# Attention bias and mask: from matmuls into the score PSUM to factors applied after the exponential

## The chip, the cores and the metric

The kernel runs on all 8 cores of one Trainium2 chip. The metric is the device time of the slowest core, in microseconds. Before the change it is 1325.45 us (median of the 3 runs made first, 1325.04 to 1452.33; with a fourth run of 1325.14 us the median is 1325.3). A program on all 8 cores has a second, slower state: one die runs at a lower granted TensorE clock and the time is some per cent longer. The 1452.33 us run was in it. (Medians are quoted over all runs of a kernel: in runs 1, 3, 5, 7, 13 and 14 below one slow run is among them. Ratios leave the slow runs out.)

## The reference, cut to what matters

One layer of a streaming encoder: a half-step feed-forward network (FFN1), a mixing stage (attention beside a convolution, joined by an output projection), a second half-step feed-forward network (FFN2), a norm. The change touches only the scores of the attention.

```python
BATCH, SEQ, D_MODEL, CHUNK, LEFT_CHUNKS = 4, 4096, 1024, 64, 8
BAND = (LEFT_CHUNKS + 1) * CHUNK   # 576 keys per chunk of 64 queries
N_HEADS, HEAD_DIM, MAX_REL = 8, 64, 128
# inside chunk_band_attention(q, k, v, rel_bias); rel_bias: (2*MAX_REL+1, N_HEADS)
idx = jnp.clip(qi + LEFT_CHUNKS * CHUNK - kj, -MAX_REL, MAX_REL) + MAX_REL
bias = jnp.transpose(rel_bias[idx], (2, 0, 1))          # (H, CHUNK, BAND)
s = jnp.einsum('bcqhd,bckhd->bchqk', qc, kb) * scale
s = s + bias[None, None]
s = jnp.where(valid, s, NEG_INF)
p = jax.nn.softmax(s, axis=-1)
o = jnp.einsum('bchqk,bckhd->bcqhd', p, vb)
```

Because exp(s + b) = exp(s) exp(b), the bias can be added before the exponential or multiplied in after it. Distances of 128 or more share one bias value. Both kernels subtract that value from the whole table, which softmax doesn't notice, so only the 256 nearest columns of the band need any work.

## The kernel before

Each core takes half of one sequence, in two groups of blocks of 512, 384 or 256 frames (even cores: 512/384/256, then 512/256/256). Per group it runs FFN1, the mixing stage, FFN2. The order of all instructions is fixed when the program is built. An emitter keeps an estimated clock for each engine and each buffer, and always emits the piece of work that it expects to be ready first.

An attention *unit* is two heads (`e` = 0, 1) times up to 4 x 128 score columns (a "bin" of key tiles, each with the queries that see it). TensorE computes the unit's scores into one of two PSUM slots. ScalarE takes their exponential into one of four bf16 buffers, `Pb`. TensorE multiplies these by the values (PV; the 65th column gives the row sum). VectorE divides by the sum into `On`, TensorE transposes `On`, and the output projection follows. The head dimension is 64, so score matmuls use half of TensorE's rows, the two heads in the two halves ("64*128" in the profile, against "128*128"). Bias and mask are matmuls of half an identity with a table, into the same PSUM slot:

```python
def qk(u):                                   # scores of one unit
    sp_ = nxt("gub", 2)                      # PSUM slot
    for (r, a, w, o_) in u["lst"]:           # key tile r, w columns
        for e in range(2):
            lhsT, kk = kslice(kt0 + r, e, j)
            ops.append((e, lhsT, qT[e*64:e*64+64, j, m0+a:m0+a+w], o_, w, ...))
    for (r, a, w, o_) in u["lst"]:           # bias and mask, by matmul
        parts = []
        if r >= 3:                           # near the diagonal: bias
            q0 = (r - 4) * 128
            for half_, lim in ((0, 192), (1, 256)):
                lo, hi = max(a, q0), min(a + w, q0 + lim)
                parts.append((half_, B_BT + j*BW + 192*half_ + lo - q0, o_ + lo - a, hi - lo))
        if r < nt:                           # a key chunk too old: NEG
            parts.append((0, B_M0, o_ + r*128 - a + 64, 64))
        for half_, tb, c_, w_ in parts:
            for e in range(2):
                z = B_ID + 64 * (1 - half_ + e)
                ops.append((e, cb[64*e:64*e+64, z:z+128], cb[64*e:64*e+64, tb:tb+w_], c_, w_, ...))
    # ... emit all ops, accumulating in PSUM
    pi = nxt("Pb", 4)
    act(Pb[pi][:, :, 0:w], src, AF.Exp, 2 * w, ...)

def pv_at():                                 # when PV of the oldest unit may come
    if c == a: return INF
    return max(P.est("pe", (("P", u["pi"]),)), ob_free() if u["bi"] == 0 else 0.0)

def evac_engine(gi):                         # who empties the PSUM of projections
    if ("attn0", gi) in F and ("attn", gi) not in F:
        return "dve"                         # during attention: always VectorE
    return "act" if P.t["act"] < P.t["dve"] else "dve"

def rdy():                                   # gate/up of an FFN (fi == 1: FFN2)
    if fi == 1 and ("attn", gi) not in F: return INF
    # ...

def keep_warm(gap, skip):                    # dummy matmuls into an expected TensorE gap
    if gap < 0.8 or gap > 100: return
    # ...
```

Projections of later blocks are emitted between the units, as filler for TensorE. The sum of squares for the next norm is squared on ScalarE and added up on GpSimd (128x512 fp32 adds) during the attention. `On` lies in memory that FFN2's gate tile uses again.

The softmax here doesn't subtract the row's maximum and nothing guards it: scores larger than these inputs give would overflow.

Of the kernel before, what the change touches and what calls it, by code (L numbers as in the profile page):

```python
# [15 lines left out]
NEG = -30000.0  # L16
# [28 lines left out]
CS_RB = CS_LNB + NG  # L45
CS_N = CS_RB + 4
BW = 448
CB_BG = 0
CB_ID = 4 * BW
CB_IC = CB_ID + 256  # L50
CB_B5 = CB_IC + CH
CB_N = CB_B5 + 128
B_BT = 0
B_ID = 4 * BW
B_M0 = B_BT + 192
B_ONES = B_ID + 256
B_ONE5 = B_ONES + 128
B_N = B_ONE5 + 128

RING_COLS = 18736  # L60
D_BYTES = 49920
# [222 lines left out]
def build_nc(debug=None):  # L284
# [20 lines left out]
    with ExitStack() as es:  # L305
# [77 lines left out]
        onesS = cb[:, B_ONES:B_ONES + 128]  # L383
        id128 = cb[:, B_ID + 64:B_ID + 192]
        ones5 = cb[:, B_ONE5:B_ONE5 + 128]

        def make(half):
# [557 lines left out]
            def ffn(g, fi):  # L945
# [5 lines left out]
                for hf, npc in ((0, 6), (1, 5)):  # L951
# [22 lines left out]
                    def rdy():  # L974
                        if fi == 1 and ("attn", gi) not in F:
                            return INF
                        c = cand()
                        return min(x[0] for x in c) if c else INF
# [43 lines left out]
                    if hf == 1:  # L1022
                        for s in blocks:
                            F.add(("hfree", gi, idx + 1, s))
                    nf = 2 * npc
                    nm = "dA" if hf == 0 else "dB"
                    if hf == 0:
# [326 lines left out]
            def attention(g):  # L1354
# [5 lines left out]
                for s in g.fine:  # L1360
# [32 lines left out]
                    def qk(u):  # L1393
                        sp_ = nxt("gub", 2)
                        u["sp"] = sp_
                        j = u["j"]
                        ops = []
                        for (r, a, w, o_) in u["lst"]:
                            for e in range(2):
                                lhsT, kk = kslice(kt0 + r, e, j)  # L1400
                                ops.append((e, lhsT, qT[e * 64:e * 64 + 64, j, m0 + a:m0 + a + w], o_, w,
                                            (kk, ("q", gi, j, s)), w / 4800.0 + 0.0025))
                        for (r, a, w, o_) in u["lst"]:
                            parts = []
                            if r >= 3:
                                q0 = (r - 4) * 128
                                for half_, lim in ((0, 192), (1, 256)):
                                    lo, hi = max(a, q0), min(a + w, q0 + lim)
                                    parts.append((half_, B_BT + j * BW + 192 * half_ + lo - q0, o_ + lo - a, hi - lo))
                            if r < nt:  # L1410
                                parts.append((0, B_M0, o_ + r * 128 - a + 64, 64))
                            for half_, tb, c_, w_ in parts:
                                for e in range(2):
                                    z = B_ID + 64 * (1 - half_ + e)
                                    ops.append((e, cb[64 * e:64 * e + 64, z:z + 128], cb[64 * e:64 * e + 64, tb:tb + w_],
                                                c_, w_, ("cb",), w_ / 4800.0 + 0.0025))
                        left = [sum(1 for x in ops if x[0] == e) for e in range(2)]
                        seen = [0, 0]
                        for (e, lhsT, rhs, o_, w, rd, dur) in ops:
                            seen[e] += 1  # L1420
                            fin = seen[e] == left[e]
                            mm(2 * sp_ + e, o_, lhsT, rhs, w, seen[e] == 1, fin, rd, fin, dur=dur)
                        pi = nxt("Pb", 4)
                        u["pi"] = pi
                        w = u["n"]
                        src = ps4[:, sp_ * 1024:(sp_ + 1) * 1024].rearrange("p (e t) -> p e t", e=2)[:, :, 0:w]
                        act(Pb[pi][:, :, 0:w], src, AF.Exp, 2 * w, (("ps", 2 * sp_), ("ps", 2 * sp_ + 1)), (("P", pi),))

                    def pv(u):
# [40 lines left out]
                    def rdy0():  # L1470
                        if ("silu", gi) not in F or ("K", gi) not in F or ("Q", gi, s) not in F or ("v", gi, s) not in F or len(mode["lru"]) < 3 and len(ob) < nb:
                            return INF
                        b = 2 * nxt("gub", 2, False)
                        return P.est("pe", (("q", gi, 0, s), ("v", gi, kt0 + nt - 1)), (("ps", b), ("ps", b + 1)))
# [15 lines left out]
                    def pv_at():  # L1490
                        if c == a:
                            return INF
                        u = units[c]
                        return max(P.est("pe", (("P", u["pi"]),)), ob_free() if u["bi"] == 0 else 0.0)
# [86 lines left out]
            def setup_tables():  # L1581
                yield lambda: P.est("dve", ("stage",)) if all(("h", 0, 0, s) in F for s in G[0].ids) else INF
                dve(lambda h: h.tensor_copy(out=cb[:, B_ID:B_ID + 256], in_=stage[:, CB_ID:CB_ID + 256]), 256,
                    ("stage",), ("cb",))
                dve(lambda h: h.tensor_scalar(out=ic_t, in0=stage[:, CB_IC:CB_IC + CH], scalar1=0.5, scalar2=None,
                                              op0=ALU.mult), CH, ("stage",), ("ic",))
                dve(lambda h: h.tensor_scalar(out=ones5, in0=stage[:, CB_B5:CB_B5 + 128], scalar1=1.0 / 512, scalar2=None,
                                              op0=ALU.mult), 128, ("stage",), ("cb5",))
                for j in range(4):
                    rbc = cs[:, CS_RB + j:CS_RB + j + 1]  # L1590
                    for lo, hi in ((0, 192), (256, BW)):
                        src = stage[:, CB_BG + j * BW + lo:CB_BG + j * BW + hi]
                        dst = cb[:, B_BT + j * BW + lo:B_BT + j * BW + hi]
                        dve(lambda h, dst=dst, src=src, rbc=rbc: h.tensor_scalar(
                            out=dst, in0=src, scalar1=rbc, scalar2=None, op0=ALU.subtract), 192,
                            ("stage", "cs"), ("cb",))
                    m_ = cb[:, B_BT + j * BW + 192:B_BT + j * BW + 256]
                    dve(lambda h, m_=m_: h.memset(m_, NEG), 64, (), ("cb",))
                    yield lambda: P.t["dve"] - 1.0
                F.add(("tables",))  # L1600

            dve(lambda h: h.memset(onesS, 1.0 / 1024), 128, (), ("cb1",))
# [82 lines left out]
def _prep_shared(inp):  # L1685
# [44 lines left out]
    rb = np.asarray(inp["rel_bias"], f)[0]  # L1730
    cs[:, CS_RB:CS_RB + 4] = np.repeat(rb[256].reshape(4, 2).T, 64, axis=0)
    out["cs"] = cs
# [5 lines left out]
    for h in range(8):  # L1738
        c0, r0 = CB_BG + (h // 2) * BW, 64 * (h % 2)
        tab = rb[dist, h]  # L1740
        cbig[r0:r0 + 64, c0:c0 + 192] = tab[0:64, 0:192]
        cbig[r0:r0 + 64, c0 + 192:c0 + BW] = tab[64:128]
    cbig[:, CB_ID + 64:CB_ID + 192] = np.eye(128, dtype=f)
    cbig[:, CB_IC:CB_IC + CH] = np.tile(np.eye(CH, dtype=f), (PH, 1))
# [54 lines left out]
```

## Time and profile before

| what | before |
|---|---|
| time, median of all four runs (fast ones alone: 1325.14) | 1325.3 us |
| even cores, odd cores, span in the profile | 1321.5 to 1323.3, 1317.3 to 1318.3 us |
| granted TensorE clock by core | 0.994 to 0.997 |
| attention stage of group 0, of group 1 (core 6) | 70.1 and 73.6 us |
| bias and mask matmuls on core 6 | 456 |

All profile lines are of core 6. It is the slowest of the eight before, after and in run 1; in run 3 it is 0.4 us and in run 12 1.8 us below the slowest. From the page: busy time of each engine, and the chain that ended last.

```profile
PE 1292.1 (98%) x8666; PEld 740.4 (56%) x8666; DVE 487.1 (37%) x899; ACT 407.0 (31%) x727; POOL 229.0 (17%) x266
...
PE 92%; DVE 3%; DMA 2%; issue 1%; ACT 1%; SPq 0%; DVEq 0%; POOL 0%; ACTq 0%; POOLq 0%
```

TensorE (PE) sets the time: the chain runs 92% through it. Now the windows of the two attention stages, each from its first score matmul to its last transposes. The columns are start:end, length, then busy time and instructions of PE, weight load, VectorE, ScalarE and GpSimd, then granted clock, DMA share and GB/s.

```profile
357.80:428.00 70.20, 69.41 (x877) 43.57 (x877) 34.19 (x81) 48.06 (x68) 12.58 (x11) 1.00 0.20 48
999.50:1073.20 73.70, 72.01 (x985) 48.12 (x985) 34.57 (x80) 53.99 (x76) 13.04 (x13) 1.00 0.17 42
```

TensorE looks full here too: 2.5 us of 143.9 are not busy. VectorE is busy for less than half, ScalarE for about 70%. The groups that the change removes (count, then busy us and mean ns of one):

```profile
L561 PE MATMUL psA<-cb_sb 64*128 64x64 bf16 x144 | 12.1, 189 | 0.0
L561 PE MATMUL psA<-cb_sb 64*128 64x256 bf16 x88 | 12.0, 269 | 0.0
L561 PE MATMUL psA<-cb_sb 64*128 64x192 bf16 x88 | 10.8, 243 | 0.0
L561 PE MATMUL psA<-cb_sb 64*128 64x128 bf16 x136 | 10.4, 216 | 0.0
```

The means are of no use as costs. A 64-column matmul shows 189 ns and a 256-column one 269 ns, because each record spans the whole pipeline and overlaps its neighbours. What a matmul costs is read from start to start. Part of the TensorE timeline (start, length, group, count):

```profile
386.38 0.39 PE L561 MATMUL psA<-dreg,at 64*128 64x384 bf16 x4
386.61 0.36 PE L561 MATMUL psA<-cb_sb 64*128 64x64 bf16 x8
386.81 0.33 PE L561 MATMUL psA<-dreg,at 64*128 64x384 bf16 x2
386.97 0.35 PE L561 MATMUL psA<-cb_sb 64*128 64x192 bf16 x4
```

The matmuls come in pairs, one for each head; the second starts 3 ns after the first. A row of this view bears the form of its first matmul only: the eight of the second row are two of 64 and six of 128 columns. They take from 386.61 to 386.81 us. In the trace itself, the 64-column pair takes 28 ns and each 128-column pair 56. Last, what TensorE waits for over the whole span (total us, times, longest), and the end of the attention of group 1:

```profile
PEld ps L561 <- issue: 19.5, 46, 2.5
...
PE ps L561 <- DVE dreg L1456: 1.5, 2, 0.8
...
PE ps L561 <- ACT pb L574: 0.5, 1, 0.5
```

```profile
1067.63 1.91 PE L561 MATMUL ps<-dreg,ring 128*128 128x256 bf16 x16 [0.30 <-DVE xres L1556]
1069.37 3.98 PE L561 MATMUL psA<-hT,ring 128*128 128x512 bf16 x16
1073.18 0.27 PE L561 MATMUL ps<-cb_sb,dreg 128*128 128x128 bf16 x2
```

PV waits for an exponential (`ACT pb`) for 0.5 us in all, and transposes wait for `On` (`DVE dreg L1456`) for 1.5 us. In the second fence, FFN2's first tile (`psA<-hT,ring`, 16 matmuls) starts at 1069.37, ahead of the last transposes at 1073.18: it fills the time in which VectorE finishes the last block.

### The profile page before, as it was taken

What the parts mean: (1) busy time and instruction counts of PE and PEld (TensorE: products, weight loads), DVE (VectorE), ACT (ScalarE), POOL (GpSimd) and SP (SyncE); (2) the same over time, 40 slices, a digit from 0 to 9 for tenths busy, and PEclk for the clock granted to TensorE, in tenths of its full rate; (3) what the DMA queues carried; (4) which work ended last, traced back from release to release, by engine and by line L of the source; (5) the groups of instructions that cost most, each with busy time, mean ns of one, the idle gap of its engine ahead of it and who ended that gap; (6) DMA issues with size and microseconds to landing.
All of it is one profiled execution on the core that took longest, in us unless ns stands there. A gap on an engine that the chain in (4) does not pass through costs nothing.

```text
span 1323.3 us, 23324 instructions; the slowest of 8 cores (1317.3 to 1323.3 us)
## 1 busy us (share of the span) xinstructions
PE 1292.1 (98%) x8666; PEld 740.4 (56%) x8666; DVE 487.1 (37%) x899; ACT 407.0 (31%) x727; POOL 229.0 (17%) x266
## 2 busy tenths in 40 slices
PE   7999999999999999999999999999999999999995
PEld 3655655566665666665564444446566664444444
DVE  4522222263745522222266222125455362222125
ACT  3411011242666421001236110114338661101123
POOL 2263000341003320000161000014120220000022
PEclk9999999999999999999999999999999999999998
DMA  8795226244930753243445844342784125433503
GB/s 187 164 217 116 49 47 120 42 127 142 193 70 2 188 91 72 53 76 53 73 52 101 218 80 82 66 76 49 171 208 103 34 39 111 75 65 64 112 0 130
DMA packets 33923, 129.55 MB, mean 98 GB/s; under 512 B 2832, under 2 KB 13200, under 8 KB 26896
## 3 DMA queue, kind: packets, MB, share of 16 engines
q0 software_dynamic: 18752, 97.33, 38.9%
q1 hardware_dynamic: 15056, 30.68, 6.8%
q8 instruction: 73, 1.20, 0.4%
q14 instruction: 42, 0.34, 0.1%
HBM read 193.54 MB, written 18.68 MB: 160 GB/s over the span
## 4 chain that ended last, share of the span: by engine, by line
PE 92%; DVE 3%; DMA 2%; issue 1%; ACT 1%; SPq 0%; DVEq 0%; POOL 0%; ACTq 0%; POOLq 0%
PE psA L561 53%; PE ps L561 39%; DVE hT L823 1%; DMA gscr_1<-dreg 1%; DMA ring<-wgu 1%; DVE xres L1048 1%; DVE xres L823 0%; DMA dreg<-gscr_1 0%; ACT L569 0%; DMA xres<-xin 0%; ACT rstd L574 0%; SPq L1673 0%; DVE xres L1556 0%; ACT pb L574 0%; POOL ssb L771 0%
## 5 line engine op out<-in xcount | busy, mean ns | idle before, releaser
L561 PE MATMUL psA<-hT,ring 128*128 128x512 bf16 (+2 forms) x3792 | 691.4, 344 | 1.7 <-DVE dreg L1139 1.0
L561 PEld LDWEIGHTS psA<-hT,ring 128*128 128x128 bf16 x3792 | 370.6, 98 | 316.1 <-issue 3.6
L574 ACT ACTIVATE dreg<-psA 128x512 f32<-128x512 f32 (+3 forms) x279 | 162.3, 587 | 688.1 <-PE psA L561 678.6
L561 PE MATMUL ps<-at,ring 128*128 128x512 bf16 (+2 forms) x1920 | 326.6, 332 | 0.0
L1014 DVE TENSOR_TENSOR at<-psA,dreg 128x512 bf16<-128x512 f32 (+2 forms) x213 | 130.1, 612 | 450.7 <-PE psA L561 427.3
L561 PEld LDWEIGHTS ps<-at,ring 128*128 128x128 bf16 x1920 | 187.6, 98 | 137.2
L1048 DVE SCALAR_TENSOR_TENSOR xres<-ps,xres 128x512 f32<-128x512 f32 (+2 forms) x160 | 88.5, 556 | 168.0 <-PE ps L561 168.0
L766 POOL TENSOR_TENSOR ssum<-ssum,sq 128x512 f32<-128x512 f32 (+2 forms) x102 | 103.2, 1012 | 169.4 <-ACT sq L574 165.6
L668 POOL DMA_DIRECT2D ring<-wgu x47 | 25.6, 546 | 522.9 <-PE ps L561 261.0
L561 PE MATMUL ps<-dreg,ring 128*128 128x256 bf16 (+4 forms) x704 | 85.7, 274 | 2.1 <-DMA dreg<-gscr_1 1.5
L574 ACT ACTIVATE sq<-xres 128x256 bf16<-128x256 f32 (+2 forms) x108 | 55.3, 519 | 99.8 <-DVE xres L1048 66.7
L823 DVE SCALAR_TENSOR_TENSOR hT<-xres,cs_sb,rstd 128x256 bf16<-128x256 f32 (+2 forms) x120 | 70.4, 644 | 12.4 <-ACT rstd L574 12.4
L561 PEld LDWEIGHTS ps<-dreg,ring 128*128 128x128 bf16 x704 | 55.2, 98 | 23.1 <-issue 4.4
L561 PE MATMUL ps<-hT,ring 128*128 128x512 bf16 (+2 forms) x352 | 63.4, 336 | 0.0
L561 PEld LDWEIGHTS ps<-hT,ring 128*128 128x128 bf16 x352 | 33.6, 98 | 25.5 <-issue 0.4
L569 ACT ACT_TABLE_LOAD x36 | 46.2, 1283 | 0.6
L574 ACT ACTIVATE pb<-psA 128x1024 bf16<-128x1024 f32 (+2 forms) x42 | 37.7, 915 | 8.1 <-PE psA L561 7.9
L1556 DVE TENSOR_TENSOR xres<-ps,xres 128x256 f32<-128x256 f32 (+2 forms) x48 | 24.9, 531 | 37.2 <-PE ps L561 37.1
L1576 POOL TENSOR_TENSOR dreg<-pb 128x2560 bf16<-128x2560 bf16 x8 | 35.8, 4502 | 0.7 <-DMA cwscr<-dreg 0.7
L668 POOL DMA_DIRECT2D ring<-wdA x16 | 8.6, 537 | 135.7 <-PE psA L561 135.3
L561 PE MATMUL ps<-at,hT 128*128 128x512 bf16 x136 | 30.8, 379 | 0.0
L561 PE MATMUL psA<-cb_sb 64*128 64x64 bf16 (+3 forms) x456 | 27.8, 223 | 0.0
(93 smaller groups left out, 588.5 us busy)
## 6 DMA issues: line engine op xcount, KB each, us to landing
ring<-wgu POOLq DMA_DIRECT2D x41, 1024.0 KB, 8.4
ring<-wdA POOLq DMA_DIRECT2D x16, 768.0 KB, 8.6
ring<-wdB POOLq DMA_DIRECT2D x16, 640.0 KB, 7.9
ring<-cwscr POOLq DMA_DIRECT2D x16, 640.0 KB, 9.7
cwscr<-dreg SPq DMA_DIRECT2D x8, 640.0 KB, 6.1
ring<-wab POOLq DMA_DIRECT2D x8, 512.0 KB, 8.2
ring<-wout POOLq DMA_DIRECT2D x4, 1024.0 KB, 14.7
dreg<-xin SPq DMA_DIRECT2D x2, 2048.0 KB, 21.9
```

Source lines behind the costliest of these rows:

```text
L561: P.op("pe", lambda h: h.matmul(o, lhsT=lhsT, rhs=rhs, start=start, stop=stop, skip_group_check=True), (max(n / 2400.0 + 0.0025, 0.03) if ...
L569: P.op("act", lambda h: h.activation(out=cs[0:1, CS_N + i:CS_N + i + 1], in_=onesS[0:1, 0:1], func=func), 1.5, ("cb1",), ())
L574: P.op("act", lambda h: h.activation(out=out, in_=in_, func=func, **kw), 0.12 + n / 1200.0 + (0.09 * sum(isinstance(v, bass.AP) for v in k ...
L668: P.dma("pool", lambda h, dst=dst, src=src: h.dma_start(out=dst, in_=src), wtok(p, i), (256 if p.reads else 512) * w, reads=p.reads, after ...
L766: pool(lambda h: h.tensor_tensor(out=ss, in0=ss, in1=sqt, op=ALU.add), n, (sk, ("sq", i)), (sk,))
L823: dve(lambda h, dst=dst, xin=xin, gcol=gcol: h.scalar_tensor_tensor(out=dst, in0=xin, scalar=gcol, in1=rt, op0=ALU.mult, op1=ALU.mult), n, ...
L1014: dve(lambda h: h.tensor_tensor(out=at, in0=ub, in1=tt, op=ALU.mult), n, (("ps", bU), ("tmpF", ti)), (("AT", gi, fl, s),))
L1048: dve(lambda h, xo=xo, xi=xi, bk=bk: h.scalar_tensor_tensor(out=xo, in0=bk, scalar=0.5, in1=xi, op0=ALU.mult, op1=ALU.add), n, (("ps", b), ...
L1556: dve(lambda h, xo=xo, bk=bk: h.tensor_tensor(out=xo, in0=bk, in1=xo, op=ALU.add), n, (("ps", b),) + rk, (("x", gi, dm, s),))
L1576: P.op("pool", lambda h, o_=o_, i0=i0: h.tensor_tensor(out=o_, in0=i0, in1=i1, op=ALU.mult), 4.5, ("cmp", "ic", "cb"), (("cwb", i % 2),))
```

## The change

Intent: TensorE sets the time, so the 456 bias and mask matmuls go. Their work moves to VectorE, which is busy for 37%. The exponentials are multiplied in place by a bf16 table `eb` = exp(bias - far bias), and masked corners are set to zero. PV of a unit may be emitted only after its multiply. As one consequence FFN2 must wait until the last transposes of its group have been emitted, since its gate tile overwrites `On`. The diff, cut to its core (left out: the new layout of the constants, that the attention also waits for `eb`, and that `eb` is set to zero where a key lies in a later chunk than the query):

```diff
                     def rdy():
-                        if fi == 1 and ("attn", gi) not in F:
+                        if fi == 1 and (("attn", gi) not in F or any(("O", gi, 3, x) not in F for x in g.fine)):
                             return INF
@@ qk
-                        for (r, a, w, o_) in u["lst"]:
-                            parts = []
-                            ... (bias and mask matmuls, as printed above)
@@ after the exponential
+                        u["ok"] = False
+                        def weigh(u=u, pi=pi, j=j, nt=nt):
+                            for (r, a, w, o_) in u["lst"]:
+                                if r >= 3:
+                                    q0 = (r - 4) * 128
+                                    lo, hi = max(a, q0), min(a + w, q0 + 256)
+                                    x = Pb[pi][:, :, o_ + lo - a:o_ + hi - a]
+                                    y = eb[:, 2 * j:2 * j + 2, lo - q0:hi - q0]
+                                    dve(lambda h, x=x, y=y: h.tensor_tensor(out=x, in0=x, in1=y, op=ALU.mult),
+                                        2 * (hi - lo), (("P", pi), "eb"), (("P", pi),), rate=1900.0)
+                                if r < nt:
+                                    c_ = o_ + r * 128 - a + 64
+                                    z = Pb[pi][0:64, :, c_:c_ + 64]
+                                    dve(lambda h, z=z: h.memset(z, 0.0), 128, (), (("P", pi),))
+                            u["ok"] = True
+                        if any(r >= 3 or r < nt for r, a, w, o_ in u["lst"]):
+                            later(lambda pi=pi: P.est("dve", (("P", pi),)) - 0.3, (), weigh)
+                        else:
+                            u["ok"] = True
@@ pv_at
-                        if c == a:
+                        if c == a or not units[c]["ok"]:
@@ setup_tables
                 # ...
+                for h_ in range(8):
+                    # ...
+                    act(eb[:, h_, :], stage[:, CB_BG + 256 * h_:CB_BG + 256 * h_ + 256], AF.Exp, 256, ("stage",), ("eb",))
+                table(AF.Silu)
                 # ...
```

More of the change, by code (lines that the diff above doesn't have):

```diff
@@ L45 @@
 CS_RB = CS_LNB + NG
-CS_N = CS_RB + 4
-BW = 448
+CS_N = CS_RB + 8
 CB_BG = 0
-CB_ID = 4 * BW
-CB_IC = CB_ID + 256
+CB_ID = 8 * 256
+CB_IC = CB_ID + 128
 CB_B5 = CB_IC + CH
@@ L53 @@
 B_BT = 0
-B_ID = 4 * BW
-B_M0 = B_BT + 192
-B_ONES = B_ID + 256
+B_ID = 8 * 256
+B_ONES = B_ID + 128
 B_ONE5 = B_ONES + 128
 B_N = B_ONE5 + 128
-RING_COLS = 18736
+RING_COLS = 18592
 D_BYTES = 49920
@@ L383, in build_nc @@
         onesS = cb[:, B_ONES:B_ONES + 128]
-        id128 = cb[:, B_ID + 64:B_ID + 192]
+        id128 = cb[:, B_ID:B_ID + 128]
+        eb = cb[:, B_BT:B_BT + 2048].rearrange("p (h t) -> p h t", h=8)
         ones5 = cb[:, B_ONE5:B_ONE5 + 128]
@@ L1025, in ffn @@
                     nf = 2 * npc
+                    F.add(("down", gi, fi))
                     nm = "dA" if hf == 0 else "dB"
@@ L1402, in qk @@
                                             (kk, ("q", gi, j, s)), w / 4800.0 + 0.0025))
-                        for (r, a, w, o_) in u["lst"]:
-                            parts = []
-                            if r >= 3:
-                                q0 = (r - 4) * 128
-                                for half_, lim in ((0, 192), (1, 256)):
-                                    lo, hi = max(a, q0), min(a + w, q0 + lim)
-                                    parts.append((half_, B_BT + j * BW + 192 * half_ + lo - q0, o_ + lo - a, hi - lo))
-                            if r < nt:
-                                parts.append((0, B_M0, o_ + r * 128 - a + 64, 64))
-                            for half_, tb, c_, w_ in parts:
-                                for e in range(2):
-                                    z = B_ID + 64 * (1 - half_ + e)
-                                    ops.append((e, cb[64 * e:64 * e + 64, z:z + 128], cb[64 * e:64 * e + 64, tb:tb + w_],
-                                                c_, w_, ("cb",), w_ / 4800.0 + 0.0025))
                         left = [sum(1 for x in ops if x[0] == e) for e in range(2)]
@@ L1470, in rdy0 @@
                     def rdy0():
-                        if ("silu", gi) not in F or ("K", gi) not in F or ("Q", gi, s) not in F or ("v", gi, s) not in F or len(mode["lru"]) < 3 and len(ob) < nb:
+                        if ("eb",) not in F or ("silu", gi) not in F or ("K", gi) not in F or ("Q", gi, s) not in F or ("v", gi, s) not in F or len(mode["lru"]) < 3 and len(ob) < nb:
                             return INF
@@ L1582, in setup_tables @@
                 yield lambda: P.est("dve", ("stage",)) if all(("h", 0, 0, s) in F for s in G[0].ids) else INF
-                dve(lambda h: h.tensor_copy(out=cb[:, B_ID:B_ID + 256], in_=stage[:, CB_ID:CB_ID + 256]), 256,
-                    ("stage",), ("cb",))
+                dve(lambda h: h.tensor_copy(out=id128, in_=stage[:, CB_ID:CB_ID + 128]), 128, ("stage",), ("cb",))
                 dve(lambda h: h.tensor_scalar(out=ic_t, in0=stage[:, CB_IC:CB_IC + CH], scalar1=0.5, scalar2=None,
@@ L1588, in setup_tables @@
                                               op0=ALU.mult), 128, ("stage",), ("cb5",))
-                for j in range(4):
-                    rbc = cs[:, CS_RB + j:CS_RB + j + 1]
-                    for lo, hi in ((0, 192), (256, BW)):
-                        src = stage[:, CB_BG + j * BW + lo:CB_BG + j * BW + hi]
-                        dst = cb[:, B_BT + j * BW + lo:B_BT + j * BW + hi]
-                        dve(lambda h, dst=dst, src=src, rbc=rbc: h.tensor_scalar(
-                            out=dst, in0=src, scalar1=rbc, scalar2=None, op0=ALU.subtract), 192,
-                            ("stage", "cs"), ("cb",))
-                    m_ = cb[:, B_BT + j * BW + 192:B_BT + j * BW + 256]
-                    dve(lambda h, m_=m_: h.memset(m_, NEG), 64, (), ("cb",))
-                    yield lambda: P.t["dve"] - 1.0
-                F.add(("tables",))
+                for h_ in range(8):
+                    src, rbc = stage[:, CB_BG + 256 * h_:CB_BG + 256 * h_ + 256], cs[:, CS_RB + h_:CS_RB + h_ + 1]
+                    dve(lambda h, src=src, rbc=rbc: h.tensor_scalar(
+                        out=src, in0=src, scalar1=rbc, scalar2=None, op0=ALU.subtract), 256,
+                        ("stage", "cs"), ("stage",))
+                    if h_ % 2:
+                        yield lambda: P.t["dve"] - 1.0
+                F.add(("tables",))
+                for h_ in range(8):
+                    yield lambda: P.t["act"] - 0.5 if ("down", 0, 0) in F else INF
+                    act(eb[:, h_, :], stage[:, CB_BG + 256 * h_:CB_BG + 256 * h_ + 256], AF.Exp, 256, ("stage",), ("eb",))
+                table(AF.Silu)
+                dve(lambda h: h.memset(eb[64:128, :, 0:64], 0.0), 512, (), ("eb",))
+                F.add(("eb",))
             dve(lambda h: h.memset(onesS, 1.0 / 1024), 128, (), ("cb1",))
@@ L1730, in _prep_shared @@
     rb = np.asarray(inp["rel_bias"], f)[0]
-    cs[:, CS_RB:CS_RB + 4] = np.repeat(rb[256].reshape(4, 2).T, 64, axis=0)
+    cs[:, CS_RB:CS_RB + 8] = rb[256]
     out["cs"] = cs
@@ L1738, in _prep_shared @@
     for h in range(8):
-        c0, r0 = CB_BG + (h // 2) * BW, 64 * (h % 2)
-        tab = rb[dist, h]
-        cbig[r0:r0 + 64, c0:c0 + 192] = tab[0:64, 0:192]
-        cbig[r0:r0 + 64, c0 + 192:c0 + BW] = tab[64:128]
-    cbig[:, CB_ID + 64:CB_ID + 192] = np.eye(128, dtype=f)
+        cbig[:, CB_BG + 256 * h:CB_BG + 256 * h + 256] = rb[dist, h]
+    cbig[:, CB_ID:CB_ID + 128] = np.eye(128, dtype=f)
     cbig[:, CB_IC:CB_IC + CH] = np.tile(np.eye(CH, dtype=f), (PH, 1))
```

## The prediction

> **What bounds the kernel now.** TensorE. The page of the slowest core (6) has PE busy 1292.1 of 1323.3 us (98%), VectorE 37%, ScalarE 31%; the chain of waits is 92% PE. Clocks are granted at 0.994 or more; even cores (half 0) are about 4 us longer than odd ones. Time falls only where PE work falls and nothing else becomes the limit.
>
> **Removed.** The bias and mask matmuls (psA from cb_sb): 456 on core 6, 440 on core 7. Their 27.8 us in the groups view overlap neighbours. From start to start of consecutive matmuls in the trace they take 45 to 46 ns each, about 20.4 us of PE time, half in each attention stage (about 358 to 428 and 1000 to 1068 us). That is 1.5% of the span and a ceiling: over 2% (26.5 us) cannot come from it.
>
> **Added.** VectorE, between exponential and PV: I count 88 bf16 multiplies on core 6 (44 of 2x256, 44 of 2x128 elements) and 52 memsets of 2x64. The trace has no bf16 tensor_tensor on VectorE. The Trainium skill ("VectorE: DVE Perf Modes", The perf-mode tier table) gives it double rate from SBUF; no run here shows it yet. Estimate from this trace: fp32-to-bf16 casts within SBUF take 427 ns at 512 and 313 ns at 288 elements, so about 0.42 and 0.29 us; memset 165 ns for 128 elements. Sum: 18.5 + 12.8 + 8.6 = 40 us, 20 per stage. At single rate (0.69 and 0.42 us) it would be 57.
> Also 8 small exponentials and a table pair on ScalarE (about 6 us, in the first down projection, where ScalarE idles), and FFN2 waits for the last transposes. Ring offsets of the weights come out unchanged.
>
> **On the critical path.** The windows view of 1000 to 1074 has PE 72.3, ACT 54.3, DVE 34.6 us busy; 358 to 430 has PE 71.0, ACT 48.1, DVE 36.0. Without bias matmuls PE needs about 62 and 61; ACT stays, DVE rises to about 55. PE stays the largest, but the slack shrinks from 20 us to below 10 and each unit's chain gains a hop of 0.3 to 0.8 us. Four P buffers and projection matmuls as filler hide most of it. Weak places: the first 512-block of group 1 (1005 to 1028 us: 20 exponentials of 1.017 us in a stretch that would shrink to 22 us), and the tail of each group (exp, multiply, PV, reciprocal, transpose, output projection in series).
> I expect 65 to 75% of 20.4 us to survive, 14 us, less 2 us for the tails and the later FFN2 start: 12 to 13 us.
>
> **Prediction: 1313 us, 8 in 10 between 1306 and 1322.** Faster by over 2%: 0.02; within 2%: 0.94; slower by over 2%: 0.04.
>
> **What would show each step.** PE matmuls down by 456 on core 6; span down about 12 us, all in the two attention stages; FFN stages of unchanged length. New VectorE multiplies of 0.42 and 0.29 us; VectorE busy up about 40 us. PV matmuls waiting on VectorE for some us in total, PE idle in the attention stages up from about 3 us to 6 to 11. ACT about 80% busy there. Odd cores gain as much.
>
> **What would make it wrong.** Multiplies at single rate: VectorE near 65 us per stage becomes the limit and delays the PSUM evacuations behind it, gain near zero. The static order, built on estimated durations, could place PV before a late multiply: stalls, at worst a loss of some us. If filler hides everything, the full 20 us: 1305.

## The result, and the profile after

The time is 1335.65 us (median of 4 runs, 1334.16 to 1337.12). The ratio after/before is 1.0079, with a 95% interval of 1.0059 to 1.0099: the change costs 10.5 us where the prediction had a gain of 12. Ratios here are the mean time of one kernel's fast runs over that of the other's fast runs in the same rounds, so they are not quite the ratios of the medians quoted. Below, "against before" means (ratio - 1) x 1325.45 us; an interval of 0.0015 to 0.0020 to either side of a ratio is 2.0 to 2.7 us.

The lines of core 6 that answer to those of before. Page:

```profile
PE 1291.2 (97%) x8243; PEld 731.5 (55%) x8243; DVE 526.4 (40%) x1030; ACT 411.5 (31%) x741; POOL 228.2 (17%) x266
...
PE 88%; DVE 4%; DMA 3%; issue 2%; ACT 1%; POOL 0%; SPq 0%; DVEq 0%; ACTq 0%; POOLq 0%
```

TensorE has 423 instructions fewer: 456 bias and mask matmuls are gone, and 33 more dummies fill gaps that the emitter foresaw (73 instead of 40). Yet its busy time fell by 0.9 us only. The attention stages:

```profile
357.20:436.70 79.50, 72.15 (x687) 40.80 (x686) 59.70 (x151) 50.36 (x74) 15.56 (x15) 0.94 0.19 45
1004.40:1079.60 75.20, 68.64 (x754) 42.09 (x754) 54.33 (x157) 54.41 (x79) 12.90 (x13) 0.98 0.17 41
```

The stages became 9.3 and 1.5 us longer. TensorE's non-busy time rose from 2.5 to 13.9 us (154.7 - 72.15 - 68.64), VectorE's busy time from 68.8 to 114.0 us, and the granted clock fell to 0.94 in the first stage and 0.98 in the second. PE busy is 140.8 us, against 141.4 before with 421 instructions more: a matmul alone in a gap shows its whole length, one in a dense stream overlaps its neighbours. The Trainium skill warns of this ("Perfetto Trace Analysis", Identifying the Most-Contended Engine: matmul busy time is no good measure of how close TensorE is to its limit, since matmuls are pipelined), and this pair of traces agrees.

The clock deserves a look of its own. Ten microseconds before and after, in the same columns:

```profile
410.00:420.00 10.00, 10.00 (x131) 6.24 (x129) 3.73 (x9) 7.38 (x11) 3.00 (x3) 1.00 0.01 2
...
410.00:420.00 10.00, 9.51 (x71) 4.72 (x66) 6.31 (x17) 5.87 (x9) 0.23 (x1) 0.66 0.01 2
```

After the change core 6 has three stretches at half clock in these stages (410.4 to 417.2, 434.3 to 437.7, 1076.0 to 1079.4 us), 13.7 us together, so up to 6.8 us of TensorE time are not granted. The other cores have less, 1.7 to 3.4 us. Before the change no core has any. So part of the 10.5 us, on most cores at most 3.4, can be the clock; no run separates it. The clock is not the main cause: run 2 below loses 17.2 us with at most 1.7 us of it in the stages of any core.

The loss is all in these stages. Each stage below runs from the first score matmul to the last transposes ("attention"), and from there to the first down projection of FFN2 ("tail"); the rest of the span is 2.5 us shorter than before (985.4 against 988.0).

| core 6, us | attention 0 | tail 0 | attention 1 | tail 1 | sum |
|---|---|---|---|---|---|
| before | 70.1 | 104.4 | 73.6 | 87.2 | 335.4 |
| after | 79.6 | 101.6 | 75.3 | 90.3 | 346.7 |

Most of the loss is in the attention of group 0. The weak place that the prediction named by its time, the first block of group 1, lies in the stage that lost 1.7 us.

What was added on VectorE (busy us, mean ns, idle before and its releaser; two of the four `Pb` buffers are called `pb` and two `dreg`):

```profile
L1425 DVE TENSOR_TENSOR pb<-pb,cb_sb 128x512 bf16<-128x512 bf16 x26 | 16.1, 623 | 1.2
L1425 DVE TENSOR_TENSOR dreg<-dreg,cb_sb 128x256 bf16<-128x256 bf16 x26 | 11.1, 427 | 1.5
L1425 DVE TENSOR_TENSOR dreg<-dreg,cb_sb 128x512 bf16<-128x512 bf16 x18 | 7.4, 417 | 1.2 <-DVE dreg L1425 0.5
L1425 DVE TENSOR_TENSOR pb<-pb,cb_sb 128x256 bf16<-128x256 bf16 x18 | 5.8, 321 | 1.2 <-ACT pb L573 0.2
L1430 DVE MEMSET dreg<- 64x128 bf16 x28 | 4.5, 165 | 1.3 <-ACT dreg L573 1.3
L1430 DVE MEMSET pb<- 64x128 bf16 x24 | 3.9, 165 | 0.5 <-ACT pb L573 0.4
```

The 18 multiplies in the third line have a mean of 417 ns; the 26 of the same form in the first have 623. The operation is the same; what differs is what GpSimd does meanwhile, as the timeline shows:

```profile
407.20 0.42 DVE L1425 TENSOR_TENSOR pb<-pb,cb_sb 128x512 bf16<-128x512 bf16 x1
...
407.74 1.15 POOL L770 TENSOR_TENSOR ssb<-ssum,sq 128x512 bf16<-128x512 f32 x1 [2.07 <-ACT sq L573]
...
407.85 1.32 DVE L1425 TENSOR_TENSOR pb<-pb,cb_sb 128x512 bf16<-128x512 bf16 x1
409.29 0.32 PEld L560 LDWEIGHTS ps<-at,pb 128*128 128x128 bf16 x8 [1.30 <-issue]
409.32 0.41 PE L560 MATMUL ps<-at,pb 128*128 128x65 bf16 x8 [1.21 <-DVE pb L1425]
```

The first multiply takes 0.42 us. The second starts while a GpSimd add is under way, takes 1.32 us and ends at 409.17, 0.28 us after the add; PV then follows 1.21 us late. The weight load of the same PV has its idle time under "issue", though what it waits for is the same multiply, so an "issue" of the weight load should be read beside the matmul's own line. On core 6, 17 of the 88 multiplies overlap such adds. The 14 that start while an add is under way are stretched (up to 1355 ns); the 3 that started before the add are not. The 71 others have means of 418 ns (2x256) and 283 ns (2x128). At these means the 88 would take 44 x 0.418 + 44 x 0.283 = 30.8 us; they take 40.6.

TensorE's waits, whole span:

```profile
PEld ps L560 <- issue: 40.4, 100, 2.5
...
PE ps L560 <- DVE pb L1425: 4.5, 7, 1.2
...
PE ps L560 <- DVE dreg L1464: 3.1, 6, 0.7
...
PE ps L560 <- DVE dreg L1425: 1.6, 3, 1.1
PE ps L560 <- DVE dreg L1430: 1.5, 2, 0.8
...
PE ps L560 <- DVE pb L1430: 1.0, 1, 1.0
```

PV waits for multiplies and memsets (4.5 + 1.6 + 1.5 + 1.0 = 8.6 us), and transposes wait twice as long for `On` (L1464, 3.1 us against 1.5). And the end of group 1:

```profile
1073.63 0.28 PE L560 MATMUL ps<-at,dreg 128*128 128x65 bf16 x4 [1.08 <-DVE dreg L1425]
...
1077.49 2.29 PE L548 MATMUL ps<-cb_sb 128*128 128x256 bf16 x11
1079.62 0.28 PE L560 MATMUL ps<-cb_sb,dreg 128*128 128x128 bf16 x2
1079.74 3.62 PE L560 MATMUL psA<-hT,ring 128*128 128x512 bf16 x16
```

FFN2's first tile now comes after the last transposes, and eleven dummies (L548) stand where it stood before.

### The profile page after: what moved, and what is told of

The parts are those of the page before. It is cut to its first block, busy times and chain, and to the rows that moved or that the text cites. A ratio compares the mean times of both kernels' runs of the same rounds, so it can differ in the third digit from the quotient of the medians.

```text
span 1332.1 us, 22727 instructions; the slowest of 8 cores (1325.7 to 1332.2 us)
## 1 busy us (share of the span) xinstructions
PE 1281.6 (96%) x8140; PEld 728.6 (55%) x8243; DVE 528.1 (40%) x1030; ACT 411.1 (31%) x741; POOL 227.6 (17%) x266
## 3 DMA queue, kind: packets, MB, share of 16 engines
q8 instruction: 70, 1.15, 0.4%
## 4 chain that ended last, share of the span: by engine, by line
PE 88%; DVE 5%; issue 3%; DMA 2%; ACT 1%; SPq 0%; DVEq 0%; ACTq 0%; POOLq 0%
PE psA L560 51%; PE ps L560 37%; DVE hT L822 2%; DMA gscr_0<-dreg 1%; DVE pb L1425 1%; DMA gscr_1<-dreg 1%; DMA ring<-wgu 1%; DVE xres L1048 0%; DVE dreg L1464 0%; ACT dreg L573 0%; DMA xres<-xin 0%; ACT L568 0%; DMA dreg<-gscr_1 0%; DVE xres L1564 0%; ACT pb L573 0%
## 5 line engine op out<-in xcount | busy, mean ns | idle before, releaser
L560 PE MATMUL psA<-hT,ring 128*128 128x512 bf16 (+2 forms) x3727 | 684.2, 344 | 4.2 <-DVE dreg L1139 0.9
L822 DVE SCALAR_TENSOR_TENSOR hT<-xres,cs_sb,rstd 128x256 bf16<-128x256 f32 (+2 forms) x120 | 70.1, 640 | 20.7 <-ACT rstd L573 20.7
L667 POOL DMA_DIRECT2D ring<-wdB x16 | 8.5, 533 | 110.7 <-PE psA L560 110.7
```

The lines of the kernel that those rows point to most:

```text
L560: P.op("pe", lambda h: h.matmul(o, lhsT=lhsT, rhs=rhs, start=start, stop=stop, skip_group_check=True), (max(n / 2400.0 + 0.0025, 0.03) if ...
L667: P.dma("pool", lambda h, dst=dst, src=src: h.dma_start(out=dst, in_=src), wtok(p, i), (256 if p.reads else 512) * w, reads=p.reads, after ...
L822: dve(lambda h, dst=dst, xin=xin, gcol=gcol: h.scalar_tensor_tensor(out=dst, in0=xin, scalar=gcol, in1=rt, op0=ALU.mult, op1=ALU.mult), n, ...
```

## The experiments

Four suspects: multiplies and memsets stand between exponential and PV (the *chain*); they take VectorE's time from PSUM evacuations, reciprocals and `On` (the *load*); GpSimd's adds stretch them (the *stretch*); FFN2 starts late (the *late FFN2*). A fifth: the emitter thinks VectorE cheaper than it is and orders badly (the *estimates*). The expectations number the theories; the text here uses these names. Runs 1 to 4, 5 to 8, 9 to 12 and 13 to 16 each shared one chip and its runs of the kernel before; differences across these go through the ratios.

### 1. e1_no_multiply_no_mask: the removal alone

Wrong: no bias and no mask. (The comparison passes it all the same; its tolerance doesn't see them with these inputs. So it is with runs 6, 7, 12 and 15. "Result right" below means that this comparison passed and that nothing was left out on purpose; a fault in the bias or the mask it would not show.)

```diff
 (after)
-                        if any(r >= 3 or r < nt for r, a, w, o_ in u["lst"]):
-                            later(lambda pi=pi: ..., (), weigh)
-                        else:
-                            u["ok"] = True
+                        u["ok"] = True
```

> The changed kernel without its multiplies and memsets on VectorE, so with the removal alone (wrong result on purpose). Theory 1, the new VectorE hop ate the gain: the full ceiling appears, about 1305 us (20 us under the kernel before, 30 us under the changed one). Rival, the removal itself frees less PE time than I worked out (the short matmuls hid weight loads): 1315 us or more.

Measured: 1320.56 us, ratio 0.9956 [0.9936, 0.9976], so -5.8 us against before; one of four runs was slow (1550). So the removal without any VectorE work brings much less than the 20.4 us that the prediction called its ceiling. Part of the rest is seen at the end of group 1:

```profile
1062.75 0.71 PE L548 MATMUL ps<-cb_sb 128*128 128x256 bf16 x5
1064.23 0.27 PE L560 MATMUL ps<-cb_sb,dreg 128*128 128x128 bf16 x2 [0.77 <-DVE dreg L1461]
1064.36 5.29 PE L560 MATMUL psA<-hT,ring 128*128 128x512 bf16 x16
```

FFN2's tile waits behind the transposes, and its 16 matmuls then take 5.29 us instead of 3.62: the window 1060 to 1070 has a granted clock of 0.83. Another part is the size of the removal itself. Start to start, the bias and mask matmuls of before sum to 21.0 us. But after the second of a 64-column pair the next matmul starts in 25 ns if it too uses half the rows, and in 122 ns if it uses all (a PV, say); after a 256-column pair in 106 and 202 ns. About 96 ns of each of the 61 such changes, 5.9 us, is the change of row mode. It was booked on the last bias matmul, and in this run it stands after the last score matmul (63 times; after a 128-column pair 148 ns instead of about 53). Score matmuls with bias and mask took 38.0 us start to start before, score matmuls alone 24.2 us here: 13.8 us are really freed. The Trainium skill ("TensorEngine Tiling (Array Packing)", Key Properties) says that a change of tiling mode drains TensorE; the trace agrees that the change costs, and puts 96 ns on it. Whether that is the drain itself is not shown: a weight load takes 95 to 98 ns in the profile too, and may merely lie open there. The way back costs the same (a half-row matmul after a PV starts in 126 ns, another PV in 32).

### 2. e2_add_only: the VectorE work on top of the matmuls

```diff
 (before, its bias and mask matmuls kept)
+    weigh() as in the change, but with a table of ones; pv_at() and the condition on FFN2 as in the change
```

> The kernel before with its bias matmuls kept, and the same multiplies (by a tile of ones), memsets and the later FFN2 start added: the addition alone, right result. If the two parts simply add, about 1325 + 30 = 1355 us. If the addition costs only because PE got faster (the stage now being bound by VectorE and the chain), it is nearly hidden here: 1328 to 1335 us.

Measured: 1343.74 us, ratio 1.0130 [1.0113, 1.0147], +17.2 us, result right. The additions cost 17.2 us where nothing was removed, and 10.5 + 5.8 = 16.3 us on top of run 1. The time lies between the two expected ones. 17.2 is near 16.3, so removal and additions nearly add up, and the additions are the larger. TensorE's filler hides little of them.

### 3. e3_small_gpsimd_adds: the stretch

Wrong (relative error 0.51): during the output projection the adds of squares touch 16 columns, with the emission order unchanged.

```diff
 (after)
-  pool(lambda h: h.tensor_tensor(out=ss, in0=ss, in1=sqt, op=ALU.add), n, ...)
+  m_ = 16 if st.get("wo") else n
+  pool(lambda h: h.tensor_tensor(out=ss[:, 0:m_], in0=ss[:, 0:m_], in1=sqt[:, 0:m_], op=ALU.add), n, ...)
```

> The changed kernel with the GpSimd adds of squares in the output projection cut to 16 columns, same order of all instructions (wrong result on purpose). Theory 2, the multiplies that meet a GpSimd add wait until it ends, and these about 10 us of VectorE time in both attention stages are on the path: multiplies all near 0.42 and 0.29 us, time 1326 to 1330 us. Rival, their lateness is hidden or is a small part: 1332 us or more.

Measured: 1331.32 us, ratio 1.0040 [1.0020, 1.0060], +5.3 us, so 5.2 us better than the change, between the two expected ranges. The groups of the multiplies that shrank:

```profile
L1426 DVE TENSOR_TENSOR pb<-pb,cb_sb 128x512 bf16<-128x512 bf16 x26 | 11.7, 454 | 1.3
...
L1426 DVE TENSOR_TENSOR dreg<-dreg,cb_sb 128x256 bf16<-128x256 bf16 x26 | 7.3, 280 | 1.5
```

From 623 to 454 ns and from 427 to 280 ns with the same operands: what stretched them was the GpSimd adds. The Trainium skill has the mechanism ("SBUF — State Buffer", Who interferes with whom): GpSimd's SBUF ports are VectorE's second pair, under an exclusive lock, and a VectorE instruction with two SBUF inputs contends with a GpSimd instruction that reads SBUF. The traces agree, down to the timing. From 283 to 418 ns, 256 more elements take 135 ns, so the data of a multiply take about 0.27 us at 512 elements and 0.135 at 256; with the change, the stretched multiplies end 0.28 and 0.15 us after the add. Their data seem to flow only once the add is done. This costs 5 us here: real, but a third of the additions' cost. Shorter adds could also help by themselves; the kernel before with its adds cut was not run. What speaks for the stretch is that core 6 gains in the attention stages (79.6 to 74.4 and 75.3 to 73.7 us) and hardly in the tails (101.6 to 101.1, 90.3 to 90.3).

### 4. e4_honest_costs: the estimates

```diff
 (after)
-  P.op("dve", fn, 0.07 + n / rate, reads, writes)
+  P.op("dve", fn, 0.15 + n / rate, reads, writes)
```

> The changed kernel, the emitter's fixed cost of a VectorE instruction raised from 0.07 to 0.15 us, near what the trace shows (0.15), so that the static order is built on truer durations. Theory 3, PV and others are placed before late VectorE work because the order was built on too short durations: 1325 to 1330 us. Rival, no order hides the hop: 1334 us or more.

Measured: 1336.14 us, ratio 1.0079 [1.0062, 1.0096]: no change. That the emitter orders badly because it thinks VectorE too cheap falls, in this form.

### 5. e5_late_ffn2_alone: only the late FFN2, added to before

```diff
 (before)
-  if fi == 1 and ("attn", gi) not in F:
+  if fi == 1 and (("attn", gi) not in F or any(("O", gi, 3, x) not in F for x in g.fine)):
```

> The kernel before with only the later FFN2 start added (FFN2 waits for the last transposes), right result. In the traces the first FFN2 tile (16 matmuls, 3.5 us) fills the tail of group 1 before the change and comes after the last transposes in the changed kernel. If that costs, 1327 to 1330 us; if other work fills the tail, 1325 to 1326 us.

Measured: 1327.72 us (five rounds), ratio 1.0007 [0.9994, 1.0020], +0.9 us, not clear of noise. In the kernel before, the condition costs little.

### 6. e6_work_off_the_chain: the load without the chain

Wrong: the same multiplies and memsets at the same places on VectorE, but on a scratch tile, and PV doesn't wait for them.

```diff
 (after)
-  u["ok"] = False
+  u["ok"] = True
-  x = Pb[pi][:, :, o_ + lo - a:o_ + hi - a]
+  x = scr[:, :, 0:hi - lo]
-  h.tensor_tensor(out=x, in0=x, in1=y, op=ALU.mult)
+  h.tensor_tensor(out=x, in0=y, in1=y, op=ALU.mult)      # the memsets go to scr too
```

> The changed kernel with the same number and sizes of VectorE multiplies and memsets at the same places, but on the table into a scratch tile, so that PV does not wait for them (wrong result on purpose). The run without them took 1320.6, the changed kernel 1335.7. If the cost is the serial hop from exponential over VectorE to PV: 1321 to 1325 us. If it is VectorE's load (PSUM evacuations queue behind): 1331 to 1336 us.

Measured: 1328.37 us, ratio 1.0014 [0.9999, 1.0029], +1.9 us. Against run 1 the load alone costs 1.9 + 5.8 = 7.7 us. Putting it on the chain costs the other 10.5 - 1.9 = 8.6 us. So neither suspect is enough alone; each has about half. The chain's half contains a part of the stretch: off the chain the 88 multiplies meet the adds less, and take 36.1 us in all on core 6 instead of 40.6. What TensorE waits for here is `On`: 7.7 us over the span, against 2.3 in run 1.

### 7. e7_memsets_only: masks without multiplies

Wrong: no bias.

```diff
 (after)
-  if r >= 3:        # the multiply
+  if r >= 30:
-  if any(r >= 3 or r < nt for r, a, w, o_ in u["lst"]):
+  if any(r < nt for r, a, w, o_ in u["lst"]):
```

> The changed kernel without the multiplies, memsets kept (wrong result on purpose: no bias). By VectorE time the memsets are 8.6 of about 49 us, so 1320.6 + 15 x 0.18 = about 1323 us. If each hop costs whatever its length, about half of the units still have one: 1327 us or more.

Measured: 1324.45 us, ratio 0.9987 [0.9970, 1.0005], -1.7 us. The 52 memsets of 165 ns, 8.6 us of VectorE, cost 4.1 us over run 1, about half of their own length. The two intervals touch, so the size is rough.

### 8. e8_own_place_for_on: the change without its condition on FFN2

Dropping the condition alone is a race, because FFN2's gate tile overwrites `On`. So `On` and its reciprocals move to memory of the convolution that is dead by then.

```diff
 (after)
-  On = carve(O_RS, 3072, BF16)...         # and rcp
+  On = carve(O_GP, 3072, BF16)...
-  if fi == 1 and (("attn", gi) not in F or any(("O", gi, 3, x) not in F for x in g.fine)):
+  if fi == 1 and (("attn", gi) not in F):
```

> The changed kernel with the normalized outputs (On) and reciprocals moved to a place of their own, so that the FFN2 wait on the last transposes can go; right result. If the later FFN2 start costs in the changed kernel too: 1330 to 1333 us. If not: 1335 to 1337 us.

Measured: 1334.53 us, ratio 1.0066 [1.0051, 1.0081], +8.7 us, result right: 1.8 us better than the change, with intervals that overlap. Late FFN2 isn't what makes the change slow.

### 9 and 10. e9_removal_half_exp, e10_before_half_exp: is ScalarE the next limit?

Wrong (relative errors 0.046 and 0.044): exponentials only for the first head of each unit, whose values PV of both heads reads; run 9 on run 1, run 10 on the kernel before, as the control.

```diff
-  act(Pb[pi][:, :, 0:w], src, AF.Exp, ...)
+  act(Pb[pi][:, 0:1, 0:w], src[:, 0:1], AF.Exp, ...)
-  Pb[pi][:, e, c_:c_ + 128]               # in pv()
+  Pb[pi][:, 0, c_:c_ + 128]
```

> The removal alone (no multiplies, no memsets), and each exponential only on the first head's half, PV of both heads reading that half; same order of all instructions (wrong result on purpose). The removal frees 13.8 us of TensorE time by the traces, 5.4 us arrived. If the pace of ScalarE's exponentials takes the rest: 1312 to 1314 us. If not: 1318 to 1321 us.

> The control: the kernel before with its exponentials halved in the same way (wrong result on purpose). If TensorE alone bounds the attention stages there, 1324 to 1326 us; if ScalarE already holds it in places, below 1323 us.

Measured: run 9 1318.08 us, ratio 0.9941 [0.9923, 0.9959], -7.8 us; run 10 1324.68 us, ratio 0.9994 [0.9976, 1.0012], -0.8 us. The kernel before doesn't notice half of the exponentials' work: it is bound by TensorE there. The removal gains 2 us more with them halved, less than its own interval (2.4 us to either side). That ScalarE takes over as the limit is not what eats the removal.

### 11. e11_six_p_buffers: more units in flight

```diff
 (after)
-  pi = nxt("Pb", 4)      # and: a - c > 3
+  pi = nxt("Pb", 6)      # and: a - c > 5
```

> The changed kernel with six P buffers and six units in flight in place of four; right result. If the hop over VectorE costs as latency, which more units in flight can hide: 1327 to 1331 us. If the cost is the order of work on VectorE and TensorE, which depth does not mend: 1334 us or more.

Measured: 1340.44 us, ratio 1.0105 [1.0087, 1.0123], +13.9 us: worse than the change, and a miss. In its profile the odd cores have 1320.6 to 1323.7 us, shorter than with the change (1325.7 to 1327.7); the even ones have 1334.7 to 1339.7, longer (1330.4 to 1332.2). A deeper queue isn't a cure. With the same instructions cores move by some 5 us either way; depth and order changed together, so this is not shown to be the order alone. Why the two halves part is open.

### 12. e12_removal_own_place: the removal alone, FFN2 free

Wrong, as run 1.

```diff
 (run 1, and On in its own place and no condition on FFN2, as in run 8)
```

> The removal alone without the later FFN2 start, normalized outputs in a place of their own (wrong result on purpose: no bias, no mask). The trace of the removal alone has the first FFN2 tile of group 1 after the last transposes and at half clock. If that is where gain was lost: 1316 to 1318 us. If not: 1320 to 1321 us.

Measured: 1315.03 us, ratio 0.9922 [0.9904, 0.9940], -10.3 us. This is what the removal brings when nothing stands in its way: three quarters of the 13.8 us freed. The late FFN2 took the other 4.5 us of run 1. So the condition costs little in the kernel before (0.9) and in the full change (1.8), both within the noise, and is dear where the attention had become short. At the end of group 1 FFN2's tile fills the gap again:

```profile
1058.85 3.40 PE L560 MATMUL psA<-hT,ring 128*128 128x512 bf16 x15
1062.09 0.28 PE L560 MATMUL ps<-cb_sb,dreg 128*128 128x128 bf16 x2
1062.20 3.62 PE L560 MATMUL psA<-hT,ring 128*128 128x512 bf16 x16
```

### 13. e13_masks_on_pe: bias by multiply, mask by matmul

Built on run 8, result right.

```diff
 (run 8)
+  if r < nt:                              # in qk(), before: half identity x NEG, 64 columns
+      for e in range(2):
+          ops.append((e, cb[64*e:64*e+64, z:z+128], cb[64*e:64*e+64, B_M0:B_M0+64], o_ + r*128 - a + 64, 64, ...))
-  dve(lambda h, z=z: h.memset(z, 0.0), 128, (), (("P", pi),))
```

> The changed kernel with the masks back on TensorE as matmuls (a 64-wide pair costs it about 27 ns, a memset costs VectorE 165 ns), bias still by multiplies, On in its own place and no FFN2 wait; right result. The memsets alone had cost 3.9 us over the removal alone: from 1334.5 to about 1330 us. To beat the kernel before it would have to be under 1325, which I do not expect.

Measured: 1328.83 us, ratio 1.0018 [0.9998, 1.0038], +2.4 us, 6.3 better than run 8. A pair of mask matmuls of 28 ns while TensorE is in that mode anyway is cheaper here than a memset of 165 ns in the chain.

### 14. e14_masks_on_pe_split_evac: and evacuations shared with ScalarE

```diff
 (run 13)
-  if ("attn0", gi) in F and ("attn", gi) not in F:
-      return "dve"
```

> As e13, and the projections' PSUM evacuations in the attention stages go to whichever of ScalarE and VectorE is free first, in place of VectorE always; right result. If VectorE load is what hurts: 1325 to 1328 us. If ScalarE is then in the way: 1330 us or more.

Measured: 1327.48 us, ratio 1.0015 [0.9995, 1.0035], +2.0 us, result right: no clear difference from run 13. Runs 13 and 14 are the best right versions with multiplies, and at best equal to the kernel before.

### 15. e15_off_chain_own_place: the load without the chain, FFN2 free

```diff
 (run 6, and On in its own place and no condition on FFN2, as in run 8)
```

> As e12 (removal, On in its own place, no FFN2 wait: 1315.0 us) with the VectorE work of the change done off the chain, on a scratch tile (wrong result on purpose). With the FFN2 wait the load alone cost 7.8 of 15.1 us. The same share here: about 1325 us. If load is all: 1333 to 1335 us; if the hop is all: 1315 to 1318 us.

Measured: ratio 0.9984 [0.9964, 1.0004], -2.1 us; three of six runs were slow, the fast ones have a mean of 1323.19 us (the median of all six, 1351.27, says nothing). Against run 12 the load costs 8.2 us. Against run 8 the chain costs 10.8. Again the wait that grows off the chain is the one for `On` (4.2 us on core 6 against 1.4 in run 12).

### 16. e16_small_adds_own_place: the stretch, FFN2 free

```diff
 (run 8, and GpSimd adds of 16 columns, as in run 3)
```

> As e8 (the changed kernel, On in its own place, no FFN2 wait: 1334.5 us) with the GpSimd adds of squares in the output projection cut to 16 columns (wrong result on purpose). With the FFN2 wait that gave back 4.4 us: about 1330 us again; 1334 if it was chance.

Measured: ratio 1.0023 [1.0007, 1.0040], +3.0 us (two of six runs slow, mean of the fast ones 1328.24 us): 5.7 us better than run 8. The stretch is the same size as in run 3.

### The sum

| step (us against before) | FFN2 free | FFN2 waits |
|---|---|---|
| freed on TensorE, from start times | -13.8 | -13.8 |
| removal alone | -10.3 (run 12) | -5.8 (run 1) |
| and VectorE's work, off the chain | -2.1 (run 15) | +1.9 (run 6) |
| and on the chain | +8.7 (run 8) | +10.5 (the change) |
| of this, GpSimd stretch | 5.7 (run 16) | 5.2 (run 3) |

The VectorE work costs 19.0 us in the left column and 16.3 in the right. With FFN2 free, core 6's stages from the first score matmul to the first down projection (335.4 us before) sum to 325.2 in run 12, 333.8 in run 15 and 342.4 in run 8: the same three steps, within 2.3 us.

## Why the prediction was wrong

It said 1313 us, 1306 to 1322; it came out at 1335.65. The sign was wrong, and the range didn't hold it.

**Right.** The places (only the attention stages and their tails changed), the counts, the size of the multiplies (0.42 and 0.29 us expected, 0.418 and 0.283 measured where GpSimd is quiet), the memset (0.165), VectorE's busy time (about +40 us expected, +39.3 measured), and that neither gain nor loss passes 2%. The double rate that it took from the Trainium skill ("VectorE: DVE Perf Modes", The perf-mode tier table, for bf16 `tensor_tensor` from SBUF) agrees with 418 ns for 512 elements; at the single rate the prediction expected 690. TensorE's non-busy time in the attention stages was expected at 6 to 11 us and was 13.9; ScalarE at about 80% busy there, and it was 63 and 72%. Odd cores were to gain as much as even ones; they lost as much (8 to 10 us in the profile).

**The step that failed: "Four P buffers and projection matmuls as filler hide most of it."** They hid little. The VectorE work costs 16.3 us in the change (run 1 to the change), 17.2 alone (run 2), 19.0 with FFN2 free (run 12 to run 8), against the 7 to 8 us that the prediction allowed for everything (20.4 less 12 to 13). About half comes from the load and half from the chain (runs 6 and 15). The prediction compared sums: 55 us of VectorE in a stage with 62 of TensorE, so slack. But VectorE was no free engine there. It alone empties the projections' PSUM during attention and makes `On`. TensorE's waits show `On` (3.1 us against 1.5), multiplies and memsets (8.6 us); a wait for an evacuation is not among them. Slack in a sum is no proof of slack in the order.

**"About 20.4 us of PE time ... a ceiling": a mis-sized term.** 13.8 us are freed. The start times that gave 45 to 46 ns per matmul include 61 changes of row mode of about 96 ns, which remain when the bias matmuls are gone. As a ceiling it held; "65 to 75% of 20.4 us" counted on 6.6 us that were never there.

**"2 us for the tails and the later FFN2 start": mis-sized, and dependent on the rest.** 4.5 us where the attention had become short (runs 1 and 12), 1.8 in the full change (run 8) and 0.9 in the kernel before (run 5), both within the noise.

**Not foreseen: the GpSimd adds,** which stretch 14 multiplies on core 6 and cost 5.2 to 5.7 us (runs 3 and 16). The prediction took its durations from casts, which have one SBUF input; the multiplies have two. The Trainium skill's page on SBUF states the rule (quoted at run 3); the prediction didn't use it.

**Named as risks.** Single rate: didn't occur. ScalarE as the next limit in the first block of group 1: with the removal alone, 2 us and within the noise (run 9); not tried with the multiplies in place. The order built on estimated durations: better estimates changed nothing (run 4), though six buffers, with the other order that they bring, moved cores by some 5 us either way (run 11).

**Open.** Which part of the load acts, evacuations or reciprocals and `On`: the waits point to `On` (runs 6 and 15), and letting ScalarE share the evacuations made no clear difference (run 14), but that was without the memsets. How the 5 us of stretch divide between load and chain. How much the stretches at half clock add. Why six buffers part the even cores from the odd. And every variant is ordered anew by the emitter, so each single difference carries an order effect of unknown size; only what two or three runs agree on is taken as shown.

## What to carry to other kernels

Before work moves from a full engine to one that is "37% busy", look at what that engine does in just that stage and who waits for it: the move here turned a dense stream on one engine into a chain over three, and cost more than it freed. The price of a removed matmul is the start-to-start time that disappears with it, not the time up to its successor, if the successor uses another row mode and the change stays. Small work in a mode that is open anyway (a 28 ns pair of mask matmuls) can be cheaper than a 165 ns instruction on an idle engine in the chain.

## What the Trainium skill lacked or had wrong

- "TensorEngine Tiling (Array Packing)", Key Properties: it says that a change of tiling mode drains TensorE, without a number. Here a change from 64-row to 128-row matmuls costs about 96 ns (25 against 122 ns after a pair of 64-column matmuls, 106 against 202 after a 256-column pair), and the way back as much (32 against 126 ns after a PV).
- "SBUF — State Buffer", Who interferes with whom: it has the rule, but no size for a multiply against an add. Here a bf16 multiply with two SBUF inputs takes up to 1355 ns instead of 418 if it starts during a 128x512 fp32 add of about 1.15 us, and ends 0.15 to 0.28 us after it. "VectorE: DVE Perf Modes", The perf-mode tier table, gives the double rate without pointing to this.
- "VectorE: DVE Perf Modes", Zero memsets can be issued as uint32: the memsets here (64 partitions x 128 bf16 elements, 165 ns) are bf16, and no run tried the shorter form.
- Nothing in it was found wrong: the lock between VectorE and GpSimd, the double rate of bf16 `tensor_tensor` and the warning about matmul busy time agree with the traces (418 ns; 140.8 against 141.4 us busy in the attention stages with 421 instructions fewer).
